# A decoder trunk on one core: the first layer's norm gain is put on the weights, and the first loads are issued in another order

## The chip, the cores and the metric

The kernel runs on one core of a Trainium2 chip. The time is the device time of one launch in microseconds (us). The engines are named as in the profile: PE is TensorE with its matmuls, PEld its weight loads, DVE is VectorE, ACT is ScalarE, POOL is GpSimd, SP is SyncE, which issues most of the DMAs.

## The reference

Four residual layers, each with an RMSNorm in front, over 256 tokens of width 1024, in float32. Layers 0 and 3 are a pooling mixer, layer 1 is a gated DeltaNet, layer 2 is latent attention.

```python
def rmsnorm(x, g):
    y = x * lax.rsqrt(jnp.mean(x * x, axis=-1, keepdims=True) + EPS)
    return y * g

def pool_mixer(h, w_in, w_grp, scale, w_out):       # w_in: 1024 x 4096
    u, gate = jnp.split(h @ w_in, 2, axis=-1)
    ...                                              # windowed means of u, one window per group
    return (p * scale * jax.nn.silu(gate)) @ w_out

for i in range(4):
    x = x + mixer[i % 3](rmsnorm(x, norm_g[i]), ...)
return rmsnorm(x, final_g)
```

The gain `g` multiplies the columns of `h`, and these are the rows of `w_in`. So `(y * g) @ w_in` is `y @ (g[:, None] * w_in)`.

## The kernel before

**Tiles.** The 256 tokens are two row tiles, `xs[0]` and `xs[1]` (128 partitions each, t=0 and t=1). The width of 1024 is eight blocks of 128 along the contraction, k=0 to 7. Every float32 operand of a matmul is split into two parts: `hi` is the value rounded to `fp32r`, `lo` the rest. One product is three matmuls: hi·hi, hi·lo, lo·hi.

**Weights** (`weights`, L97). A DMA on SP's queue brings `raw`, one k (256 KB) or two (512 KB). ACT writes `whi` with a copy that rounds (L117), DVE writes `wlo` as `raw - whi` (L119). For the k's in the list `pool` it is POOL that writes `wlo`. A ring holds nine pairs, and `raw` has three buffers. The weights of the first gate come one k at a time, k=0 to 5 through `prefetch`, k=6 and 7 in `project`.

**Norm** (`Normed`, `LayerIn`). ACT sums the squares (L209), POOL makes the factor `xr` of each row (L245, L247, L296). `gain_tile` loads the gain spread over all partitions, in two halves (L276). DVE writes `h = x * xr * gain` (L303). For t=1 POOL makes a part of it early as `hg = x * gain` (L291), and ACT puts the factor on it (L308). PE turns `h` (L323), ACT and DVE split it into `hTh` and `hTl` (L195, L200).

**The start.** PE does 24 transposes of `ident` (L270) while the loads come in. Then follows the gate of group 3 with the tokens on the partitions (L167: for each t, eight k's of three matmuls over 512 columns). All the later gates and `u` of layer 0 have the channels on the partitions (L127 to L129: 12 matmuls over 256 columns for each k).

**The gated DeltaNet of layer 1** (below: the GDN). `substitution` solves 32x32 triangles row by row on POOL, 31 pairs of L726 and L730, on data that DMAs bring from DRAM (`d_l` to `Lb`). The result `Tb` goes to DRAM as `d_t` (L732) and comes back as `T` in eight DMAs (L736). PE needs `T` in `pairs` (L806). While POOL works, PE does the input projections of the layer: `values` (turned at L778), `queries`, and the gate of group 2, called g2 below, with 48 matmuls of L167. Two of g2's `wlo` parts, k=3 and k=7, are made by POOL.

**Order.** A scheduler sets the order of instructions on each engine by a model of their times. The program gives dependencies, and `later(...)` names instructions after which something may be issued. So a change at the start can change the order far behind it.

Of the kernel before, what the change touches and what calls it, by code (L numbers as in the profile page):

```python
# [8 lines left out]
F32 = mybir.dt.float32  # L9
# [33 lines left out]
def trunk(ctx: ExitStack, tc: tile.TileContext, x, positions, norm_g, pool_w_in, pool_w_grp,  # L43
# [3 lines left out]
    nc = tc.nc  # L47
    PSUM = bass.MemoryType.PSUM

    WARM = 24  # L50
    FREE = 4
    EARLY = 6
    E0 = 2
# [19 lines left out]
    def worka(name, *dims):  # L73
        return wa.tile([P, *dims], F32, tag="wa", name=name)
# [7 lines left out]
    def bank(pool, name):  # L82
        return pool.tile([P, CW], F32, tag=name, name=name)
# [10 lines left out]
    ready = []  # L94
    held_back = {"free": 0, "after": []}

    def weights(src, n, cols, raw=None, pool=()):  # L97

        if raw is None:
            raw = rawp.tile([P, KU * CW], F32, tag="raw", name="raw")  # L100
        m = n * cols
        dst = raw[:, :m]
        if len(src.shape) == 3:
            dma = nc.sync.dma_start(out=dst.rearrange("p (k c) -> p k c", k=n), in_=src)
        else:
            dst = dst.rearrange("p (k a b) -> p k a b", k=n, a=src.shape[2])
            for k in range(n):
                dma = nc.sync.dma_start(out=dst[:, k], in_=src[:, k])
        parts = []
        for k in range(n):  # L110
            v = raw[:, k * cols:(k + 1) * cols]
            lo = ring.tile([P, CW], F32R, tag="wlo", name="wlo")[:, :cols]
            hi = ring.tile([P, CW], F32R, tag="whi", name="whi")[:, :cols]
            held = held_back["free"] <= 0
            held_back["free"] -= 1
            with later(*(held_back["after"] if held else ())):
                a = nc.scalar.copy(hi, v)  # L117
                e = nc.gpsimd if k in pool else nc.vector
                b = e.tensor_tensor(out=lo, in0=v, in1=hi.bitcast(F32), op=ALU.subtract)  # L119
# [9 lines left out]
        nc.tensor.matmul(o, lhsT=lhs[1], rhs=rhs[0], start=False, stop=stop)  # L129

    def project(src, ks, act, cols=CW, chan=False, tail=0, done=None, cuts=1,
                where="acc", pool=()):

        first, last = ks[0][0], sum(ks[-1]) - 1  # L140

        def unit(k0, n):
            return weights(src(k0, n), n, cols,
                           pool=[a for a in range(n) if (k0 + a) % KD in pool])

        if chan:
            banks = [bank(acc if where == "acc" else aux, where) for _ in range(2)]
            for k0, n in ks:
                parts = unit(k0, n)
                for j in range(n):  # L150
                    k = k0 + j
                    for c in range(cols // P):
                        w = [v[:, c * P:(c + 1) * P] for v in parts[j]]
                        o = banks[c // 2][:, (c % 2) * S:(c % 2 + 1) * S]
                        mm3(o, w, act(k, 0, S), k == first and c % 2 == 0,
                            k == last and c % 2 == 1)
            return banks
        width = cols // cuts
        banks = [[bank(acc, "acc") for _ in range(cuts)] for _ in range(NT)]

        def rows(t, c, k0, n, parts):
            o, sl = banks[t][c][:, :width], slice(c * width, (c + 1) * width)
            for x, y in ((0, 0), (0, 1), (1, 0)) if n == 1 else ((0, None), (1, 0)):
                for j in range(n):
                    k = k0 + j
                    for z in (0, 1) if y is None else (y,):
                        nc.tensor.matmul(o, lhsT=act(k, t * P, P)[x], rhs=parts[j][z][:, sl],  # L167
                                         start=k == first and x == z == 0,
                                         stop=k == last and x == 1)
# [83 lines left out]
    def load_x(t):  # L253
        for c in range(2):
            sl = slice(c * CW, (c + 1) * CW)
            nc.sync.dma_start(out=xs[t][:, sl], in_=x[0, t * P:(t + 1) * P, sl])

    load_x(0)
    neghalf = const.tile([P, 2], F32, name="neghalf")
    nc.gpsimd.memset(neghalf, -0.5)  # L260
# [5 lines left out]
    warm = small("warm", 2, bufs=1)  # L266
    nc.scalar.activation(warm, neghalf, AF.Silu)
    ps = bank(tps, "tp")
    for _ in range(WARM):
        nc.tensor.transpose(ps[:, :P], ident, ident)  # L270

    def gain_tile(row, between):
        g = gp.tile([P, D], F32, tag="gain", name="gain")
        for c in range(2):
            sl = slice(c * CW, (c + 1) * CW)
            nc.sync.dma_start(out=g[:, sl], in_=row[:, sl].to_broadcast([P, CW]))  # L276
            if c == 0 and between:
                between()
        return g

    class Normed:

        def __init__(self, row, between=None):
            self.g, self.early = gain_tile(row, between), {}

        def begin(self, t, a):
            sl = slice(a, a + CUT)
# [4 lines left out]
        def rest(self, t):  # L294
            r = small("xr", 1)
            mark["pool"] = nc.gpsimd.tensor_tensor(out=r, in0=ms[t], in1=neghalf[:, :1],  # L296
                                                   op=ALU.pow).ins
            hs = []
            for a in range(0, D, CW):
                h = wh.tile([P, CW], F32, tag="h", name="h")  # L300
                cut = CUT if (t, a) in self.early else 0
                sl = slice(a + cut, a + CW)
                nc.vector.scalar_tensor_tensor(out=h[:, cut:], in0=xs[t][:, sl], scalar=r[:, 0:1],  # L303
                                               in1=self.g[:, sl], op0=ALU.mult, op1=ALU.mult)
                hs.append(h)
                if not cut:
                    continue
                mark["rest"] = nc.scalar.activation(h[:, :CUT], self.early.pop((t, a)), AF.Copy,  # L308
                                                    scale=r[:, 0:1]).ins
            return hs  # L310

    class LayerIn(Normed):


        def __init__(self, i, between=None):
            super().__init__(norm_g[i:i + 1, :], between)
            self.hT = Split("hT", KD)

        def feed(self, t):
# [91 lines left out]
    def pool_layer(i, j, hT):  # L411
        yT = Split("yT", POOL_W // P)
        order = (3, 2, 1, 0)

        def gate(g):
            ks = [(k, 1) for k in range(KD)] if g == order[0] and i == 0 else units(KD)
            banks = project(cols_of(pool_w_in[j], POOL_W + g * CW), ks, hT, chan=g != order[0])
            gs = [worka("gs", CW) for _ in range(NT)]
            for t in range(NT):
                nc.scalar.activation(gs[t], banks[t], AF.Silu)  # L420
            return gs

        def pooled(g):
            w = WINDOWS[g]
            banks = project(cols_of(pool_w_in[j], g * CW), units(KD), hT, chan=True)
# [770 lines left out]
    def prefetch(k, pool=()):  # L1196
        ready.append(weights(first(k, 1), 1, CW, worka("raw", CW), pool))
# [12 lines left out]
    for k in range(1, E0):  # L1210
        prefetch(k)
    start(0)
    held_back["free"] = 0
# [39 lines left out]
```

## Time and profile before

| | us |
|---|---|
| median of 3 runs | 859.88 (859.83 to 860.01) |
| the profiled execution | 859.14 |
| its span in the trace | 857.4 |

The span is the time from the first to the last instruction in the trace; 1.7 us of the profiled execution lie around it. Times of the trace count from the span's start. In rows of the timeline stand start, length (the last to end of the merged ones), engine, line, operation, output and inputs, and in brackets how long the engine had been idle and what ended that.

### The profile page before, as it was taken

The page shows a single profiled execution, that of the slowest core. Times are in us where ns is not written, and L with a number is a line of the kernel's source. Part 1 is how long each engine was busy: PE and PEld are TensorE (multiplying, and loading weights), DVE is VectorE, ACT ScalarE, POOL GpSimd, SP SyncE. Part 2 cuts the span into 40 slices and gives each one's busy share as a digit, 9 for nine tenths or more (in the row PEclk, how much of TensorE's full clock was granted, in tenths as well). Part 3 has the DMA queues.
Part 4 walks back from the last instruction along what each step waited for, and adds up shares of the span by engine and source line. Part 5 has one row for each costly group of instructions (what it writes and reads, how often), then busy time and mean ns, then how long its engine had stood idle before and what let it go on. Part 6 is the DMA issues. An engine that isn't in the chain of part 4 may idle for free.

```text
span 857.4 us, 16137 instructions
## 1 busy us (share of the span) xinstructions
PE 835.0 (97%) x5967; PEld 778.7 (91%) x5967; DVE 591.2 (69%) x1138; ACT 488.2 (57%) x1007; POOL 155.7 (18%) x292
## 2 busy tenths in 40 slices
PE   7999999999999969999999999999999999999996
PEld 6999998988999959888979998999989989999986
DVE  4589776456989665656577659778767668866852
ACT  5565555467857435555565654566555476555542
POOL 4000000233248941022212002000000210000012
PEclk9999999999999989999999999999999999999999
DMA  6765556546555462222547676743652547565551
GB/s 199 249 188 188 178 189 213 180 148 206 188 160 176 134 168 102 75 74 99 173 147 215 201 165 172 196 132 95 171 167 79 173 149 218 175 192 183 187 200 50
DMA packets 111288, 140.43 MB, mean 164 GB/s; under 512 B 23340, under 2 KB 53224, under 8 KB 111208
## 3 DMA queue, kind: packets, MB, share of 16 engines
q1 hardware_dynamic: 109056, 138.17, 53.1%
q8 instruction: 47, 0.77, 0.4%
q0 software_dynamic: 320, 1.06, 0.3%
q10 hardware_dynamic: 1832, 0.16, 0.2%
q14 instruction: 33, 0.27, 0.1%
HBM read 137.79 MB, written 1.58 MB: 163 GB/s over the span
## 4 chain that ended last, share of the span: by engine, by line
PE 85%; POOL 7%; DVE 2%; DMA 2%; issue 2%; ACT 1%; SPq 1%; POOLq 0%; ACTq 0%; DVEq 0%
PE acc L167 34%; PE acc L127 12%; PE acc L128 12%; PE acc L129 12%; POOL Tb L730 2%; POOL pr L726 2%; PE aux L127 2%; PE aux L128 2%; PE aux L129 2%; DVE h L303 1%; DMA gain<-in_norm_g_dram 1%; PE aux L688 1%; ACT junk L209 1%; PE aux L806 1%; PE tp L1165 1%
## 5 line engine op out<-in xcount | busy, mean ns | idle before, releaser
L119 DVE TENSOR_TENSOR wlo<-raw,whi 128x512 fp32r<-128x512 f32 (+1 forms) x491 | 338.6, 712 | 163.2 <-ACT whi L117 160.9
L117 ACT CAST whi<-raw 128x512 fp32r<-128x512 f32 (+1 forms) x508 | 301.4, 617 | 261.8 <-PE acc L167 89.8
L127 PE MATMUL acc<-hTh,whi 128*128 128x256 f32 x832 | 235.3, 283 | 1.0 <-DVE cv L636 1.0
L128 PE MATMUL acc<-hTl,whi 128*128 128x256 f32 x832 | 235.8, 283 | 0.0
L129 PE MATMUL acc<-hTh,wlo 128*128 128x256 f32 x832 | 234.7, 282 | 0.0
L127 PEld LDWEIGHTS acc<-hTh,whi 128*128 128x128 f32 x832 | 157.7, 190 | 1.8 <-issue 1.4
L128 PEld LDWEIGHTS acc<-hTl,whi 128*128 128x128 f32 x832 | 157.6, 189 | 0.4
L129 PEld LDWEIGHTS acc<-hTh,wlo 128*128 128x128 f32 x832 | 157.5, 189 | 0.2
L167 PE MATMUL acc<-wlo,yTh 128*128 128x256 f32 (+1 forms) x384 | 116.2, 319 | 0.0
L167 PE MATMUL acc<-whi,yTh 128*128 128x256 f32 (+1 forms) x384 | 116.2, 323 | 0.0
L167 PE MATMUL acc<-whi,yTl 128*128 128x256 f32 (+1 forms) x384 | 92.4, 321 | 0.0
L167 PEld LDWEIGHTS acc<-wlo,yTh 128*128 128x128 f32 x384 | 72.0, 188 | 5.0
L167 PEld LDWEIGHTS acc<-whi,yTh 128*128 128x128 f32 x384 | 71.9, 188 | 5.2
L167 PEld LDWEIGHTS acc<-whi,yTl 128*128 128x128 f32 x384 | 63.1, 188 | 5.6
L291 POOL TENSOR_TENSOR hg<-x,gain 128x256 f32<-128x256 f32 x18 | 14.8, 832 | 259.1 <-DVE x L353 257.4
L167 PE MATMUL acc<-wlo,hTh 128*128 128x512 f32 (+1 forms) x144 | 55.9, 394 | 0.4 <-DVE wlo L119 0.2
L167 PE MATMUL acc<-whi,hTh 128*128 128x512 f32 (+1 forms) x144 | 55.5, 393 | 0.7 <-ACT hTh L195 0.7
L167 PE MATMUL acc<-whi,hTl 128*128 128x512 f32 (+1 forms) x144 | 45.4, 388 | 0.0
L119 POOL TENSOR_TENSOR wlo<-raw,whi 128x512 fp32r<-128x512 f32 x17 | 23.1, 1360 | 70.2 <-ACT whi L117 70.2
L434 POOL COPY win<-u 128x4 f32<-128x4 f32 x8 | 2.8, 354 | 177.0 <-ACT u L428 177.0
L167 PEld LDWEIGHTS acc<-wlo,hTh 128*128 128x128 f32 x144 | 27.3, 190 | 6.8 <-DVE wlo L119 1.7
L167 PEld LDWEIGHTS acc<-whi,hTh 128*128 128x128 f32 x144 | 27.3, 190 | 6.8 <-ACT hTh L195 1.7
(337 smaller groups left out, 1443.3 us busy)
## 6 DMA issues: line engine op xcount, KB each, us to landing
raw<-in_pool_w_in_dram SPq DMA_DIRECT2D x60, 512.0 KB, 4.4
raw<-in_gdn_w_in_dram SPq DMA_DIRECT2D x48, 512.0 KB, 3.9
raw<-in_pool_w_out_dram SPq DMA_DIRECT2D x32, 512.0 KB, 3.7
raw<-in_mla_w_in_dram SPq DMA_DIRECT2D x24, 512.0 KB, 4.4
raw<-in_mla_w_uq_dram SPq DMA_DIRECT2D x36, 256.0 KB, 3.8
raw<-in_pool_w_grp_dram SPq DMA_DIRECT2D x16, 512.0 KB, 4.2
raw<-in_gdn_w_out_dram SPq DMA_DIRECT2D x16, 512.0 KB, 3.5
raw<-in_mla_w_ukv_dram SPq DMA_DIRECT2D x32, 256.0 KB, 3.4
```

What stands on the lines that cost most here:

```text
L117: a = nc.scalar.copy(hi, v)
L119: b = e.tensor_tensor(out=lo, in0=v, in1=hi.bitcast(F32), op=ALU.subtract)
L127: nc.tensor.matmul(o, lhsT=lhs[0], rhs=rhs[0], start=start, stop=False)
L128: nc.tensor.matmul(o, lhsT=lhs[0], rhs=rhs[1], start=False, stop=False)
L129: nc.tensor.matmul(o, lhsT=lhs[1], rhs=rhs[0], start=False, stop=stop)
L167: nc.tensor.matmul(o, lhsT=act(k, t * P, P)[x], rhs=parts[j][z][:, sl], start=k == first and x == z == 0, stop=k == last and x == 1)
L209: nc.scalar.activation(junk[:, :n], src, AF.Square, scale=scale, accum_out=o)
L291: nc.gpsimd.tensor_tensor(out=self.early[t, a], in0=xs[t][:, sl], in1=self.g[:, sl], op=ALU.mult)
L303: nc.vector.scalar_tensor_tensor(out=h[:, cut:], in0=xs[t][:, sl], scalar=r[:, 0:1], in1=self.g[:, sl], op0=ALU.mult, op1=ALU.mult)
L688: nc.tensor.matmul(ps[:, b], lhsT=kT[hf][:, b, tt], rhs=rhs[hf][:, b, tt], start=True, stop=True)
L726: nc.gpsimd.tensor_tensor(out=pv, op=ALU.mult, in0=Lb[:, r, r + 1:, None].to_broadcast([M * Q, n, c]), in1=Tb[:, r:r + 1, :c].to_broadcast ...
L730: nc.gpsimd.tensor_tensor(out=tv, in0=tv, in1=pv, op=ALU.subtract)
```

## The change

For layer 0 the gain is no longer put on `h`. It is loaded as eight rows of 128 on ACT's DMA queue (`grow`), turned by PE between the warming transposes, and copied by DVE to `gain0`, one column for each k. ACT's rounding copy becomes an activation with that column as scale, and DVE's subtraction becomes `raw * gain - whi`. All splits of layer 0's input weights are done in this way: 8 k's in each of 8 groups, 64. POOL no longer takes the split of k=0. `h` of layer 0 is `x * xr` alone, for t=1 too. `gain_tile` is not called for layer 0. The loads on SP are kept in the order of the program: both halves of `x` for t=0, the weights k=0 to 3, `x` for t=1, then the other weights. Other layers keep their code.

```diff
-    WARM = 24
+    WARM = 22
+    GROW = 13
...
-                a = nc.scalar.copy(hi, v)
-                e = nc.gpsimd if k in pool else nc.vector
-                b = e.tensor_tensor(out=lo, in0=v, in1=hi.bitcast(F32), op=ALU.subtract)
+                if gains is not None:
+                    a = nc.scalar.activation(hi, v, AF.Copy, scale=gains[:, k:k + 1])
+                    b = nc.vector.scalar_tensor_tensor(out=lo, in0=v, scalar=gains[:, k:k + 1],
+                                                       in1=hi.bitcast(F32), op0=ALU.mult,
+                                                       op1=ALU.subtract)
+                else:
+                    a = nc.scalar.copy(hi, v)
+                    e = nc.gpsimd if k in pool else nc.vector
+                    b = e.tensor_tensor(out=lo, in0=v, in1=hi.bitcast(F32), op=ALU.subtract)
...
+    grow = const.tile([KD, P], F32, name="grow0")
+    nc.scalar.dma_start(out=grow, in_=norm_g[0].rearrange("(k p) -> k p", p=P))
     load_x(0)
...
-    for _ in range(WARM):
-        nc.tensor.transpose(ps[:, :P], ident, ident)
+    for n in range(WARM):
+        in_order(nc.tensor.transpose(ps[:, :P], ident, ident))
+        if n == GROW:
+            pg = bank(tps, "tp")
+            in_order(nc.tensor.transpose(pg[:, :KD], grow, ident[:KD, :KD]))
+            gain0 = const.tile([P, KD], F32, name="gain0")
+            gains_in = nc.vector.tensor_copy(gain0, pg[:, :KD]).ins
...
+                if self.g is None:
+                    with later(gains_in):
+                        nc.vector.tensor_scalar(h, xs[t][:, a:a + CW], r[:, 0:1], None, ALU.mult)
+                    hs.append(h)
+                    continue
...
-            for a in range(0, D, CW):
-                if t:
-                    nxt.begin(t, a)
             nxt.feed(t)
...
-    nxt = LayerIn(0, lambda: prefetch(0, (0,)))
-    for k in range(1, E0):
+    nxt = LayerIn(0)
+    for k in range(E0):
         prefetch(k)
```

**The order at the start.** SP's queue before (a row is a DMA; `x_93` is t=0, `x_94` is t=1):

```order
L256 DMA x_93<-in_x_dram 128x512 x2
L276 DMA gain<-in_norm_g_dram 128x512
L104 DMA raw<-in_pool_w_in_dram 128x512
L276 DMA gain<-in_norm_g_dram 128x512
L104 DMA raw<-in_pool_w_in_dram 128x512 x3
L256 DMA x_94<-in_x_dram 128x512 x2
L104 DMA raw<-in_pool_w_in_dram 128x512 x2
```

SP's queue now:

```order
L271 DMA x_93<-in_x_dram 128x512 x2
L110 DMA raw<-in_pool_w_in_dram 128x512 x4
L271 DMA x_94<-in_x_dram 128x512 x2
L110 DMA raw<-in_pool_w_in_dram 128x512 x4
L110 DMA raw<-in_pool_w_in_dram 128x2x512 x12
```

The two loads of the gain are gone, and the weights k=0 to 3 stand right behind `x` of t=0.

DVE's first rows before (`h` is the normed input, `wlo` a weight's low part, `hTl` that of the turned input):

```order
L303 SCALAR_TENSOR_TENSOR h<-x_93,xr,gain 128x512 x2
L119 TENSOR_TENSOR wlo<-raw,whi 128x512
L200 TENSOR_TENSOR hTl_169<-tp,hTh_168 128x4x128
L200 TENSOR_TENSOR hTl_178<-tp,hTh_177 128x4x128
L119 TENSOR_TENSOR wlo<-raw,whi 128x512 x2
L303 SCALAR_TENSOR_TENSOR h<-x_94,xr,gain 128x256 x2
L119 TENSOR_TENSOR wlo<-raw,whi 128x512
L200 TENSOR_TENSOR hTl_169<-tp,hTh_168 128x4x128
```

DVE's first rows now:

```order
L292 COPY gain_127<-tp 128x8
L323 TENSOR_SCALAR h<-x_93,xr 128x512 x2
L127 SCALAR_TENSOR_TENSOR wlo<-raw,gain_127,whi 128x512 x2
L215 TENSOR_TENSOR hTl_170<-tp,hTh_169 128x4x128
L215 TENSOR_TENSOR hTl_179<-tp,hTh_178 128x4x128
L127 SCALAR_TENSOR_TENSOR wlo<-raw,gain_127,whi 128x512 x6
L404 MEMSET rows 128x128
L323 TENSOR_SCALAR h<-x_94,xr 128x512 x2
```

All eight weight splits of the first gate now stand ahead of `h` of t=1; before, three did on DVE, with POOL's one. On PE all 24 matmuls of t=0 now come ahead of the transposes for t=1, where 12 did before.

**The order in the GDN.** No line of it is changed, but the scheduler moved its parts. POOL, in the second half of the substitution before (L726 and L730 are the chain, L119 the splits of g2 for k=3 and k=7):

```order
L730 TENSOR_TENSOR Tb<-Tb,pr 64x12x20
L119 TENSOR_TENSOR wlo<-raw,whi 128x512
L726 TENSOR_TENSOR pr<-Lb,Tb 64x231
L730 TENSOR_TENSOR Tb<-Tb,pr 64x11x21
L726 TENSOR_TENSOR pr<-Lb,Tb 64x220
L730 TENSOR_TENSOR Tb<-Tb,pr 64x10x22
L726 TENSOR_TENSOR pr<-Lb,Tb 64x207
L730 TENSOR_TENSOR Tb<-Tb,pr 64x9x23
L726 TENSOR_TENSOR pr<-Lb,Tb 64x192
L119 TENSOR_TENSOR wlo<-raw,whi 128x512
L730 TENSOR_TENSOR Tb<-Tb,pr 64x8x24
```

POOL at the end of the substitution now (L754 and L758 are the chain, L133 the splits):

```order
L133 TENSOR_TENSOR wlo<-raw,whi 128x512
L754 TENSOR_TENSOR pr<-Lb,Tb 64x135
L758 TENSOR_TENSOR Tb<-Tb,pr 64x5x27
L754 TENSOR_TENSOR pr<-Lb,Tb 64x112
L758 TENSOR_TENSOR Tb<-Tb,pr 64x4x28
L754 TENSOR_TENSOR pr<-Lb,Tb 64x87
L758 TENSOR_TENSOR Tb<-Tb,pr 64x3x29
L754 TENSOR_TENSOR pr<-Lb,Tb 64x60
L758 TENSOR_TENSOR Tb<-Tb,pr 64x2x30
L754 TENSOR_TENSOR pr<-Lb,Tb 64x31
L133 TENSOR_TENSOR wlo<-raw,whi 128x512
L758 TENSOR_TENSOR Tb<-Tb,pr 64x31
```

The first split stood ahead of step 64x231 of the chain and stands now ahead of step 64x135, six pairs of steps later; the second stood within step 64x192 and stands now within the last step.

SP's queue around the way of `T` through DRAM before:

```order
L104 DMA raw<-in_gdn_w_in_dram 128x2x512 x15
L732 DMA d_t<-Tb 64x1024
L104 DMA raw<-in_gdn_w_in_dram 128x2x512
L736 DMA T<-d_t 32x8x32 x8
L104 DMA raw<-in_gdn_w_in_dram 128x2x512 x2
```

And now:

```order
L110 DMA raw<-in_gdn_w_in_dram 128x2x512 x13
L760 DMA d_t<-Tb 64x1024
L764 DMA T<-d_t 32x8x32
L110 DMA raw<-in_gdn_w_in_dram 128x2x512
L764 DMA T<-d_t 32x8x32 x4
L110 DMA raw<-in_gdn_w_in_dram 128x2x512
L764 DMA T<-d_t 32x8x32 x3
L110 DMA raw<-in_gdn_w_in_dram 128x2x512 x3
```

Two weight loads fewer are issued ahead of `d_t`, and two stand between the loads of `T`. On PE, between the last matmul of L688 (which feeds the substitution) and L806, 299 matmuls of L127 to L129 and the 48 of g2 stood before; now it is 276 and the 48. The other 23 come behind L806.

More of the change, by code (lines that the diff above doesn't have):

```diff
@@ L95, in trunk, with in_order, weights @@
     held_back = {"free": 0, "after": []}
-    def weights(src, n, cols, raw=None, pool=()):
+    def in_order(ins):
+        return tc.keep_in_program_order(ins)
+    def weights(src, n, cols, raw=None, pool=(), gains=None):
         if raw is None:
@@ L104, in weights @@
             dma = nc.sync.dma_start(out=dst.rearrange("p (k c) -> p k c", k=n), in_=src)
+            if gains is not None:
+                in_order(dma)
         else:
@@ L131, in project @@
     def project(src, ks, act, cols=CW, chan=False, tail=0, done=None, cuts=1,
-                where="acc", pool=()):
+                where="acc", pool=(), gains=None):
         first, last = ks[0][0], sum(ks[-1]) - 1
@@ L143, in unit @@
             return weights(src(k0, n), n, cols,
-                           pool=[a for a in range(n) if (k0 + a) % KD in pool])
+                           pool=[a for a in range(n) if (k0 + a) % KD in pool],
+                           gains=None if gains is None else gains[:, k0:k0 + n])
         if chan:
@@ L255, in load_x @@
             sl = slice(c * CW, (c + 1) * CW)
-            nc.sync.dma_start(out=xs[t][:, sl], in_=x[0, t * P:(t + 1) * P, sl])
+            in_order(nc.sync.dma_start(out=xs[t][:, sl], in_=x[0, t * P:(t + 1) * P, sl]))
+    grow = const.tile([KD, P], F32, name="grow0")
+    nc.scalar.dma_start(out=grow, in_=norm_g[0].rearrange("(k p) -> k p", p=P))
     load_x(0)
@@ L268, in trunk, with gain_tile @@
     ps = bank(tps, "tp")
-    for _ in range(WARM):
-        nc.tensor.transpose(ps[:, :P], ident, ident)
-    def gain_tile(row, between):
+    for n in range(WARM):
[5 more added lines that the diff above has]
+            gains_in = nc.vector.tensor_copy(gain0, pg[:, :KD]).ins
+    def gain_tile(row):
         g = gp.tile([P, D], F32, tag="gain", name="gain")
@@ L276, in gain_tile, with __init__ @@
             nc.sync.dma_start(out=g[:, sl], in_=row[:, sl].to_broadcast([P, CW]))
-            if c == 0 and between:
-                between()
         return g
     class Normed:
-        def __init__(self, row, between=None):
-            self.g, self.early = gain_tile(row, between), {}
+        def __init__(self, row):
+            self.g, self.early = None if row is None else gain_tile(row), {}
         def begin(self, t, a):
@@ L312, in trunk, with __init__ @@
     class LayerIn(Normed):
-        def __init__(self, i, between=None):
-            super().__init__(norm_g[i:i + 1, :], between)
+        def __init__(self, i):
+            super().__init__(norm_g[i:i + 1, :] if i else None)
             self.hT = Split("hT", KD)
@@ L413, in pool_layer @@
         order = (3, 2, 1, 0)
+        gains = None if i else gain0
         def gate(g):
             ks = [(k, 1) for k in range(KD)] if g == order[0] and i == 0 else units(KD)
-            banks = project(cols_of(pool_w_in[j], POOL_W + g * CW), ks, hT, chan=g != order[0])
+            banks = project(cols_of(pool_w_in[j], POOL_W + g * CW), ks, hT, chan=g != order[0],
+                            gains=gains)
             gs = [worka("gs", CW) for _ in range(NT)]
@@ L424, in pooled @@
             w = WINDOWS[g]
-            banks = project(cols_of(pool_w_in[j], g * CW), units(KD), hT, chan=True)
+            banks = project(cols_of(pool_w_in[j], g * CW), units(KD), hT, chan=True, gains=gains)
             u = big("u", 4, S)
@@ L1194, in trunk, with prefetch @@
     first = cols_of(pool_w_in[0], POOL_W + (len(WINDOWS) - 1) * CW)
-    def prefetch(k, pool=()):
-        ready.append(weights(first(k, 1), 1, CW, worka("raw", CW), pool))
+    def prefetch(k):
+        ready.append(weights(first(k, 1), 1, CW, worka("raw", CW), gains=gain0[:, k:k + 1]))
     def start(t):
```

1 line of the change is left out of this document (added).

## The prediction

> **What bounds the kernel now.** I read the page's busy shares and its chain first, then PE's waits, then the timeline of the two places where PE waits.
>
> ```profile
> span 857.4 us, 16137 instructions
> PE 835.0 (97%) x5967; PEld 778.7 (91%) x5967; DVE 591.2 (69%) x1138; ACT 488.2 (57%) x1007; POOL 155.7 (18%) x292
> PE 85%; POOL 7%; DVE 2%; DMA 2%; issue 2%; ACT 1%; SPq 1%; POOLq 0%; ACTq 0%; DVEq 0%
> ...
> PE aux L806 <- DMA T<-d_t: 7.4, 1, 7.4
> PE tp L323 <- DVE h L303: 3.0, 2, 1.6
> PE tp L323 <- ACT h L308: 1.0, 1, 1.0
> ```
>
> PE is the bound, 97% busy. A gain must come from the 22.4 us without PE, or from matmuls at less than full clock. POOL's 7% of the chain is the substitution in the GDN, ended by the longest wait, 7.4 us. The waits at L323 are the start. The span is 857.4, the execution 859.14, the median 859.88; I work out differences in the trace and put them on the median.
>
> ```profile
> 1.96 5.15 PE L270 MATMUL tp<-ident 128*128 128x128 f32 x24 [1.96 <-POOL ident masks.py:199]
> 3.46 0.63 ACT L209 ACTIVATE junk<-x 128x512 f32<-128x512 f32 x1 [1.17 <-DMA x<-in_x_dram]
> 5.36 0.57 POOL L296 TENSOR_TENSOR xr<-ms,neghalf 128x1 f32<-128x1 f32 x1
> 7.63 0.75 DVE L303 SCALAR_TENSOR_TENSOR h<-x,xr,gain 128x512 f32<-128x512 f32 x1 [7.63 <-DMA gain<-in_norm_g_dram]
> 8.19 0.62 ACT L117 CAST whi<-raw 128x512 fp32r<-128x512 f32 x1 [3.25 <-DMA raw<-in_pool_w_in_dram]
> 8.44 0.66 PE L323 MATMUL tp<-ident,h 128*128 128x128 f32 x4 [1.34 <-DVE h L303]
> 9.16 1.53 DVE L303 SCALAR_TENSOR_TENSOR h<-x,xr,gain 128x512 f32<-128x512 f32 x1 [0.78 <-DMA gain<-in_norm_g_dram]
> 10.27 0.58 ACT L195 CAST hTh<-tp 128x512 fp32r<-128x512 f32 x1
> 11.51 0.78 PE L167 MATMUL acc<-whi,hTh 128*128 128x512 f32 x1
> 16.49 1.10 PE L323 MATMUL tp<-ident,h 128*128 128x128 f32 x8 [1.01 <-ACT h L308]
> 17.39 0.98 PE L167 MATMUL acc<-whi,hTh 128*128 128x512 f32 x2
> 18.67 0.40 PE L167 MATMUL acc<-whi,hTl 128*128 128x512 f32 x1
> 18.91 0.40 PE L167 MATMUL acc<-whi,hTh 128*128 128x512 f32 x1
> ```
>
> The reader sees that the row factor is ready at 5.93, but `h` starts at 7.63 and 9.16, when the gain's halves land. From 17.39 PE always has work. By then it has done 12 of the 48 matmuls of the first gate.
>
> **The start, worked out.** Removed: two gain loads (256 KB each), two `hg` on POOL, two `h` halves on ACT, a 1.26 us split on POOL, two warming transposes. Added: one 4 KB load, one small transpose, one copy.
>
> PE warms until about 6.8 (22 transposes of 0.215 from 1.96, and the small one). `h` needs the factor (5.93) and `gain0`. For that I need the new load and the landing of the weights:
>
> ```profile
> raw<-in_pool_w_in_dram SPq DMA_DIRECT2D x8, 256.0 KB, 6.1
> x<-in_x_dram SPq DMA_DIRECT2D x4, 256.0 KB, 4.6
> L1047 DVE TENSOR_SCALAR ckv<-ckv,mrr 128x512 f32<-128x512 f32 x2 | 0.9, 475 | 0.0
> L200 DVE TENSOR_TENSOR yTl<-ym,yTh 128x256 fp32r<-128x256 f32 x16 | 6.7, 418 | 0.8 <-ACT yTh L195 0.5
> L202 DVE SCALAR_TENSOR_TENSOR yTl<-tp,colsT,yTh 128x256 fp32r<-128x256 f32 x24 | 10.4, 477 | 4.9 <-ACT yTh L197 4.8
> 60.00:80.00 20.00, 20.00 (x149) 18.90 (x148) 18.84 (x36) 13.32 (x25) 2.00 (x3) 1.00 0.56 177
> ```
>
> `grow`, issued at about 0.85, lands between 3.4 (the first `x`, 3.46, took 2.6 from the start of issue) and 7.0 (6.1 after issue, as weights do). I take 4, as nothing is ahead of it. Its transpose comes after 14 warming ones, at 4.97, so `gain0` is there at 5.4. With 7.0, PE's last eight warm until 8.8: 2.0 later.
>
> Then: `h` 5.95 to 6.9 (two of 0.475; before 0.75 and 1.53). Transposes 6.8 to 7.9. Weights k=0, 1 land right behind `x`, 5 to 6 (at the latest 1.71 + 6.1 = 7.8), ACT splits them before `hTh` at 7.45 and 8.05. First matmul at about 8.05, against 11.51. From there DVE sets the pace: `hTl` until 9.35, then six splits of 0.65. Those for k=4 to 7 come at the earliest 2.6 after their issue, which waits for the split of k=0 (7.5): 10.1, at the latest 13.6. I take 11. The last split ends at 14.5 to 15.4 and PE's t=0 at about 15.2. `h` of t=1 is behind the eight splits on DVE and its squares behind three on ACT: 14.6 to 15.5. Transposes, the SiLU of t=0 and three DMA issues stand ahead of `hTh` on ACT. PE is then at work without a break from 16.6 to 17.1.
>
> Sum: 17.39 less 16.85 is 0.55. PE has done 24 matmuls instead of 12, at 0.235 (18.67 to 18.91) 2.8. The first five after 17.39 took 1.28 instead of 0.94: 0.3. Start: **-3.65**. With the late landings (2.0 or 2.6 more) it is -1.2, with the early ones -4.6.
>
> What is late next at the start is DVE with the splits, then PE itself. SP passes two gain issues less, 0.9 us.
>
> **The splits of layer 0.** 64 become scalar_tensor_tensor. On 128x256 this takes 477 against 418 ns, so I add 0.06 each, 3.8 us on DVE in all; ACT's activation with a scale I take at the same. The tightest stretch is 60 to 80: DVE is busy 18.84 of 20. A k lasts PE 12 x 0.119 = 1.43, so 14 splits add 0.84, and 1.16 are free. The ring of nine covers delays within. Cost 0 to 0.84 (3.8 if nothing covered), I take 0.2.
>
> **The GDN, which only moves.** All times here are those of before; the earlier start shifts them together.
>
> ```profile
> 291.55 0.40 PE L167 MATMUL acc<-whi,hTh 128*128 128x512 f32 x1
> 293.13 1.28 POOL L119 TENSOR_TENSOR wlo<-raw,whi 128x512 fp32r<-128x512 f32 x1
> 295.05 0.40 PE L167 MATMUL acc<-wlo,hTh 128*128 128x512 f32 x1
> 298.81 1.29 POOL L119 TENSOR_TENSOR wlo<-raw,whi 128x512 fp32r<-128x512 f32 x1
> 302.86 0.82 POOL L730 TENSOR_TENSOR Tb<-Tb,pr 64x156 f32<-64x156 f32 x1
> 303.76 0.83 POOL L726 TENSOR_TENSOR pr<-Lb,Tb 64x135 f32<-64x135 f32 x1
> 262.99 0.42 POOL L726 TENSOR_TENSOR pr<-Lb,Tb 64x135 f32<-64x135 f32 x1
> 309.54 0.23 POOL L726 TENSOR_TENSOR pr<-Lb,Tb 64x31 f32<-64x31 f32 x1
> 310.12 0.47 SPq L732 DMA_DIRECT2D d_t<-Tb  x1
> 313.12 3.78 SPq L736 DMA_DIRECT2D T<-d_t  x8
> 308.45 0.28 PE L129 MATMUL acc<-hTh,wlo 128*128 128x256 f32 x1
> 316.09 3.65 PE L806 MATMUL aux<-T,LT 128*128 128x64 f32 x16 [7.36 <-DMA T<-d_t]
> 316.10:324.40 8.30, 8.30 (x41) 8.30 (x41) 4.88 (x6) 3.13 (x8) 0.00 (x0) 0.51 0.68 205
> 324.40:332.00 7.60, 7.60 (x75) 7.60 (x72) 4.67 (x9) 5.67 (x14) 0.00 (x0) 1.00 0.13 38
> ```
>
> The reader sees POOL's chain end at 310.1, `T` after it, and PE idle from 308.7 to 316.09; then 8.3 us at a granted clock of 0.51, which cost another 4.1.
>
> Now POOL comes to the split of k=3 only after the step that ended at 303.68; without the two splits, that is 301.1, so it is done at 302.4. PE wants it 3.5 us into g2, at 295.05, or some 2.5 later where `values` are turned earlier than now. So PE gets a **new wait of 5 to 7 us on POOL**, then 24 matmuls (5.6, to 308.0), a second wait for k=7 until 309.8 (309.54 + 0.23, the two splits counted within), 9 matmuls and 16 smaller ones (4.0), and the rest of the wait for `T`. POOL's chain holds the same work, so `T` comes at 316.1, plus one load between its first four, 0.45. Behind the waiting PE nothing but its own work is queued; ACT and DVE wait for its turned tiles.
>
> Price, part by part. 23 matmuls of 0.119 move behind L806, where PE is full: +2.7. `T` later: +0.5. The idle time is now in three pieces with work between, the last about 2.3, so I expect the slow clock before L806, where the wait for `T` hides it: -4.1 (0 if it comes again). Weight loads that stood ahead of `d_t` come behind it, and turned tiles are freed on ACT behind those weights: a load takes 4, and PE has 1.3 of work there, so I add 2.5 (0 to 3). DVE is idle in this stretch for want of weights, and POOL was faster then: 0.42 for step 64x135 at 262.99, 0.83 at 303.76. Some ten steps at 0.1 to 0.3 less: -1 (0 to -3). GDN: **+0.6**, between -2.5 and +5.
>
> The Trainium skill ("TensorE: Matmul & The Clock Gate", section "Part 1: The HAM clock gate (the "warmup" mystery)") gives the half clock after at least one idle window of about 3.4 us, and the full one after a busy window as long. The trace has it after a longer wait than that, 7.36, and for longer, 8.3. By the rule the new wait of 5 us alone would halve the clock, which falls into time that `T` hides; my sum would be the same. It would change only where the last piece exceeds 3.4, the second rival.
>
> Layers 2 and 3 and the output keep their code and, but for local exchanges, their order; I take 0, within 0.5.
>
> Sum: -3.65 + 0.2 + 0.6 = -2.85, **857.0 us**.
>
> **Rivals.**
> - *The GDN gives too.* Speaks for it: POOL's fast steps. Then GDN is -2.0 instead of +0.6, 854.4.
> - *Slower: the new waits on POOL cost the clock twice.* The last wait for `T` is long as well, and L806 again runs at half clock (4.1), with two weight loads ahead of the second half of `T` (0.9). GDN +5.6, sum +2.15, 862.0. It decides from a GDN price of 3.45 on; speaks for it that this wait did halve the clock before; against it that work now stands between.
> - *Late loads.* The gain rows or the weights k=4 to 7 land as late as 6.1 after issue. Start -1.2, 859.5. Speaks for it the row of the eight weight loads; against it that these stood behind the gain, which is gone.
> - *The gain's wait was hidden.* PE's matmuls start earlier, but are done no sooner, as DVE's eight splits set the pace: start -0.55, 860.1. Against it: then PE would wait between them, and the 2.8 of work done are still done.
>
> **Chances.** 857.0: 0.46. GDN gives too: 0.19. Late loads: 0.17. Hidden wait: 0.08. Slower: 0.10. The range of the likeliest is 855.5 to 858.5. The range for 8 in 10 runs from 854.0 (the second case's 854.4 less the 0.5 of the other layers) to 860.4, above the third and fourth case. A change of 0.2%, 1.7 us, is about what can be told from none: faster is below 858.16. The first two cases are faster but for 0.03, the late loads fall within: faster 0.65, same 0.26, slower 0.09.
>
> **What would show it.** In the profile after: no gain row ahead of `h`, the first L182 at about 8, PE without a break from about 17 with all of t=0 behind it. A wait of PE on POOL's `wlo` of 4 us or more in g2. L806 within 2 us of its old distance from L688, at full clock. PE's waits in layer 0 stay below 1. I am wrong if the first matmul comes after 10, if L806 runs at 0.5, or if layer 0 shows waits on `wlo` of over 2 us.

## The result: 873.9 us, slower by 1.7%, and the profile after

| | us | ratio to before |
|---|---|---|
| before | 859.86 | |
| after | 873.9 (873.3 to 874.0) | 1.0168 (1.0152 to 1.0184) |
| profiled execution after | 873.31, span 871.6 | |

A fourth run of the changed kernel took 1655.86 us, in a slow state that no profile shows, and is left out of the range and the ratio.

The forecast was 857.0 with 860.4 as its upper end. The time lies 13.5 us above that. The start became faster, as forecast; all of the loss lies in layers 1 and 2, whose code is not touched.

The page after: the line of the span, the busy shares, and the shares of the chain that ended last.

```profile
span 871.6 us, 16132 instructions
...
PE 840.2 (96%) x5966; PEld 777.4 (89%) x5966; DVE 596.4 (68%) x1140; ACT 494.4 (57%) x1005; POOL 152.4 (17%) x289
...
PE 63%; POOL 7%; DMA 3%; DVE 3%; ACT 2%; issue 2%; SPq 0%; POOLq 0%; ACTq 0%; DVEq 0%
```

PE is without work for 31.4 us (871.6 less 840.2) instead of 22.4. That explains 9 of the 14 us. The other 5 stand in PE's row as busy. Nearly 3 of them lie in the state chain and layer 2, where PE counts as busy 1.1 and 1.8 us longer for as many matmuls (821 and 1470, before 823 and 1470) at the full granted clock; I take them for waits shorter than the view shows. The rest lies ahead of the state chain, in part at half clock behind the first wait below. The longest waits of PE after (line waited for: total, times, longest):

```profile
PE acc L141 <- DVE vc L664: 4.7, 1, 4.7
PE aux L834 <- DMA T<-d_t: 4.5, 1, 4.5
PE tp L287 <- POOL ident masks.py:199: 2.0, 1, 2.0
PE acc L182 <- DVE wlo L133: 1.8, 3, 1.0
PE aux L897 <- ACT gsg L584: 1.7, 1, 1.7
PE tp L943 <- DVE yg L934: 1.6, 1, 1.6
...
PE acc L182 <- POOL wlo L133: 1.3, 1, 1.3
```

The waits for `h` at the start are gone. A wait of 4.7 on `vc` is new: `vc` is what DVE's convolution makes of the products of `values`, and PE waits until it has read a bank of `acc`. New too are waits of 1.7 and 1.6 in the state chain, the part of the GDN behind the substitution that goes head by head (`state`, `unseen`, `second`, `output`; its products stand in `aux`).

The start after, in PE's timeline:

```profile
5.13 0.27 PE L290 MATMUL tp<-ident,grow 8*128 8x8 f32 x1
...
6.93 1.04 PE L349 MATMUL tp<-ident,h 128*128 128x128 f32 x8
8.21 0.50 PE L182 MATMUL acc<-whi,hTh 128*128 128x512 f32 x1 [0.24 <-ACT hTh L210]
...
15.07 0.50 PE L182 MATMUL acc<-whi,hTh 128*128 128x512 f32 x1 [0.37 <-ACT whi L126]
...
16.43 1.04 PE L349 MATMUL tp<-ident,h 128*128 128x128 f32 x8
17.82 0.50 PE L182 MATMUL acc<-whi,hTh 128*128 128x512 f32 x1 [0.35 <-ACT hTh L210]
```

The first matmul of the gate is at 8.21 instead of 11.51, and all 24 of t=0 are done before t=1 is turned.

Where time is won and lost is seen from five marks on PE: the first matmul of L595 (layer 1; L567 before), the first with `T` (L834), the first of the state chain (L897), the first turn of `ckv` (layer 2), the last four turns of `h` (layer 3). The table gives their starts in the trace before, and how much later (+) or earlier (-) they are in the others; e1 to e4 and e10 are kernels of the next section.

| | layer 1 | T | state chain | layer 2 | layer 3 | span |
|---|---|---|---|---|---|---|
| before | 183.42 | 316.09 | 359.55 | 490.31 | 695.36 | 857.4 |
| after | -2.5 | -0.2 | +3.1 | +9.8 | +14.3 | +14.2 |
| e1, new, banks 6 and 4 | -2.3 | -2.3 | -3.4 | -3.4 | -3.3 | -3.4 |
| e2, old, banks 4 and 2 | -0.1 | -3.8 | +6.3 | +12.2 | +16.7 | +16.7 |
| e3, new, banks 4 and 4 | -2.0 | +0.6 | +2.5 | +2.5 | +3.9 | +3.9 |
| e4, new, banks 6 and 2 | -3.0 | -1.6 | -1.4 | +2.6 | +9.7 | +9.0 |
| e10, old, two banks of tp | +0.9 | -1.0 | +7.6 | +13.9 | +18.0 | +18.1 |

Each trace is of a single run: e1's took 1.1 us less than the median of its kernel, e10's 3.0 more, the others at most 0.8 off.

Layer 0 gives 2.5. The GDN up to `T` loses 2.3, from there to the state chain 3.3 (26 matmuls more stand there, 329 against 303), the state chain and what follows to layer 2 6.7, layer 2 4.5; layer 3 and the output nothing.

### The profile page after: what moved, and what is told of

Same layout as the page of the kernel before. It is cut to its first block, busy times and chain, and to the rows that moved or that the text cites. A ratio compares the mean times of both kernels' runs of the same rounds, so it can differ in the third digit from the quotient of the medians.

```text
span 871.6 us, 16132 instructions
## 1 busy us (share of the span) xinstructions
PE 840.2 (96%) x5966; PEld 777.4 (89%) x5966; DVE 596.4 (68%) x1140; ACT 494.4 (57%) x1005; POOL 152.4 (17%) x289
## 4 chain that ended last, share of the span: by engine, by line
PE 63%; POOL 7%; DMA 3%; DVE 3%; ACT 2%; issue 2%; SPq 0%; POOLq 0%; ACTq 0%; DVEq 0%
PE acc L182 24%; PE acc L142 9%; PE acc L143 9%; PE acc L141 9%; POOL pr L754 2%; POOL Tb L758 2%; PE aux L141 1%; PE aux L142 1%; PE aux L143 1%; DVE wlo L133 1%; ACT junk L224 1%; PE aux L716 1%; PE aux L834 1%; DMA raw<-in_pool_w_in_dram 1%; PE tp L1193 1%
## 5 line engine op out<-in xcount | busy, mean ns | idle before, releaser
L131 ACT CAST whi<-raw 128x512 fp32r<-128x512 f32 (+1 forms) x444 | 264.3, 617 | 240.2 <-PE acc L182 93.0
L133 DVE TENSOR_TENSOR wlo<-raw,whi 128x512 fp32r<-128x512 f32 (+1 forms) x428 | 295.4, 713 | 149.7 <-ACT whi L131 145.1
L182 PE MATMUL acc<-whi,yTh 128*128 128x256 f32 (+1 forms) x384 | 114.1, 323 | 1.7 <-ACT yTh L212 1.4
L182 PE MATMUL acc<-whi,yTl 128*128 128x256 f32 (+1 forms) x384 | 89.8, 319 | 0.0
L126 ACT ACTIVATE whi<-raw,gain 128x512 fp32r<-128x512 f32 x64 | 44.5, 722 | 28.0 <-DMA raw<-in_pool_w_in_dram 11.0
L127 DVE SCALAR_TENSOR_TENSOR wlo<-raw,gain,whi 128x512 fp32r<-128x512 f32 x64 | 46.4, 748 | 13.5 <-ACT whi L126 12.0
```

Of the source, the lines that this page charges most:

```text
L126: a = nc.scalar.activation(hi, v, AF.Copy, scale=gains[:, k:k + 1])
L127: b = nc.vector.scalar_tensor_tensor(out=lo, in0=v, scalar=gains[:, k:k + 1], in1=hi.bitcast(F32), op0=ALU.mult, op1=ALU.subtract)
```

## The cause: how many PSUM banks each pool may use

PSUM is the memory that PE writes its products to, and a bank holds one tile of 128x512 here. The kernel writes no number of buffers for its three PSUM pools `tp` (turned tiles), `acc` (projections) and `aux` (all else). A planner in the build chooses them, within eight banks. It begins with the fewest banks with which the program can run at all, and raises the limits of those pools that hold work up in its model. A pool may share its banks with another when the other needs none, so the limits can add up to more than eight.

| the build's report | tp | acc | aux | sum |
|---|---|---|---|---|
| before, first step | 1 | 4 | 2 | 7 |
| before, final | 2 | 6 | 4 | |
| after, first step and final | 2 | 4 | 2 | 8 |

The change brings a small transpose (L290) between the warming ones, with a bank of `tp` of its own. The warming transposes behind it still write to theirs. So two banks of `tp` must exist from the first step on, all eight are taken, and no PSUM pool has room to be raised. The one limit that the planner then tried to raise, that of `hg`, bought nothing in its model, and it stopped at 2, 4 and 2. The order of layers 1 and 2, which I had read as the scheduler's answer to an earlier start, is its answer to these limits.

What two banks of `aux` less do in the state chain is seen in 31 us of it, before, after and in e1 (stretch and its length; busy time and count of PE, PEld, DVE, ACT and POOL; granted clock, DMA share, GB/s):

```profile
359.50:390.50 31.00, 30.94 (x149) 26.06 (x148) 18.60 (x41) 19.15 (x56) 8.45 (x24) 1.00 0.17 52
```

```profile
362.70:393.70 31.00, 26.43 (x121) 20.57 (x121) 16.43 (x35) 14.64 (x42) 5.33 (x16) 1.00 0.16 52
```

```profile
356.00:387.00 31.00, 30.94 (x148) 26.07 (x147) 18.51 (x41) 19.25 (x56) 8.45 (x24) 1.00 0.16 52
```

PE does 121 matmuls instead of 149 in the same time, and no engine is busier for it. I read it so: each step of a head waits until DVE, ACT or POOL have emptied a bank. The view names such waits only in part (in e4, where `aux` alone is small, one of 0.6 on DVE's `vn`, two of 0.5 on `st`, one of 0.4 on `yg`); that they go with the limit is shown by e1 and e4.

What two banks of `acc` less do is seen around 266 us after. First PE's rows at the wait, then four of DVE's rows in it, then the windows (the granted clock is the third number from the end):

```profile
265.06 0.28 PE L143 MATMUL acc<-hTh,wlo 128*128 128x256 f32 x1
270.06 0.55 PE L141 MATMUL acc<-hTh,whi 128*128 128x256 f32 x1 [4.72 <-DVE vc L664]
270.41 0.42 PE L142 MATMUL acc<-hTl,whi 128*128 128x256 f32 x1
```

```profile
265.85 1.29 DVE L133 TENSOR_TENSOR wlo<-raw,whi 128x512 fp32r<-128x512 f32 x2 [0.34 <-ACT whi L131]
267.06 1.65 DVE L664 SCALAR_TENSOR_TENSOR vc<-acc,tap,vc 128x254 f32<-128x254 f32 x4
268.62 0.90 DVE L133 TENSOR_TENSOR wlo<-raw,whi 128x512 fp32r<-128x512 f32 x1
269.44 1.64 DVE L664 SCALAR_TENSOR_TENSOR vc<-acc,tap,vc 128x253 f32<-128x253 f32 x4
```

```profile
266.00:268.00 2.00, 0.00 (x0) 0.00 (x0) 2.00 (x5) 2.00 (x6) 2.00 (x4) 1.00 0.61 230
268.00:270.00 2.00, 0.00 (x0) 0.00 (x0) 2.00 (x5) 0.31 (x1) 1.84 (x5) 0.90 0.77 219
270.00:272.00 2.00, 1.94 (x9) 1.97 (x10) 2.00 (x6) 1.26 (x2) 1.76 (x4) 0.50 0.11 43
272.00:274.00 2.00, 2.00 (x15) 2.00 (x15) 2.00 (x6) 0.10 (x1) 1.76 (x4) 0.75 0.00 0
```

PE has no bank for the next product until DVE has run the convolution on the last one, between splits of weights. Behind the wait come some 3 us at half clock. The wait is there in all kernels with 4 banks for `acc` (4.7 in e2 and e10, 5.4 in e3), and in none with 6.

The Trainium skill ("Perfetto Trace Analysis", section "Matmul Optimizations") advises to use all eight PSUM banks. Both kernels do by the build's report, 16384 bytes of each partition; the runs show that the share of each pool decides too.

## The experiments

**e1: the change with the old limits.**

```diff
-    acc = ctx.enter_context(tc.tile_pool(name="acc", space=PSUM))
+    acc = ctx.enter_context(tc.tile_pool(name="acc", bufs=6, space=PSUM))
-    aux = ctx.enter_context(tc.tile_pool(name="aux", space=PSUM))
+    aux = ctx.enter_context(tc.tile_pool(name="aux", bufs=4, space=PSUM))
```

> The changed kernel with the limits of its PSUM pools written down as the planner had chosen them for the kernel before: at most 6 banks for acc and 4 for aux (in the changed kernel the planner had chosen 4 and 2). Theory P (the loss comes from the two smaller limits, which reorder layers 1 and 2): the order of layers 1 to 3 on every engine is that of before again, so the lead of 2.5 us with which layer 1 begins in the trace after is kept to the end: 859.9 - 2.5 = 857.4, within 0.7; PE's wait of 4.7 on DVE's vc and the waits in the state chain are gone, the wait for T is 7 us again. Rival S (layer 0's scaled splits or the earlier start disturb what follows, whatever the banks): stays at 868 or above, as the lead had been lost by 316 us before the state chain began.

856.8, ratio 0.9966 (0.9953 to 0.9979). Theory P holds: behind layer 0 the order is that of before but for a few rows, the new waits are gone, and `T` is waited for as before:

```profile
PE aux L834 <- DMA T<-d_t: 7.2, 1, 7.2
PE tp L287 <- POOL ident masks.py:199: 2.0, 1, 2.0
PE acc L182 <- ACT hTh L210: 1.3, 5, 0.3
PE acc L141 <- DVE cv L664: 0.8, 1, 0.8
```

**e2: the kernel before with the small limits** (`bufs=4` and `bufs=2`, nothing else).

> The kernel before with the two smaller limits, 4 banks for acc and 2 for aux, and nothing of the change. Theory P: all of the loss behind layer 0 comes without the change: in the trace after, the lead at layer 1 was 2.5 and the end 14.3 behind, so 16.7 are lost; 859.9 + 16.7 = 876.6, within 2, with the loss in the same places (by the wait for T 2.3, from there to the end of layer 1 10, in layer 2 4.4). Rival S: stays within 3 us of 859.9.

875.2, ratio 1.0173 (1.0155 to 1.0192). The loss comes without the change. Its places are those expected but for `T`, which came earlier here (-3.8); the 10.1 between `T` and the state chain take that back.

**e3 and e4: one limit each** (`acc` 4 with `aux` 4, and `acc` 6 with `aux` 2).

> The changed kernel with 4 banks for acc and 4 for aux: only aux is given back. Theory A (aux, which holds the products of the GDN's state chain and of the heads of layer 2, carries the losses there): the 7.4 lost between 357 and 402 and the 4.4 of layer 2 come back, 873.9 - 11.8 = 862.1, within 2. Theory C (acc carries them, because the projections that fill PE's time run out of banks): 868 to 872.

> The changed kernel with 6 banks for acc and 2 for aux: only acc is given back. Theory A: the losses of the state chain and of layer 2 stay, and what is lost before the wait for T and from there to 357 (2.3 + 2.8) may come back: 869 to 874. Theory C: 860 to 864.

862.8 (1.0029, 1.0019 to 1.0039) and 868.3 (1.0095, 1.0080 to 1.0111). Against e1, the small `acc` costs 6.0 and the small `aux` 11.5, together 17.5; both at once cost 17.1 (873.9 less 856.8). In e3 the loss lies ahead of the state chain and only 1.4 in layer 2; in e4 it is the state chain (4.0) and layer 2 (7.1). Theory A is right on the larger part; e4 came out 0.7 below its range of 869 to 874.

**e10 and e9: the one bank.** In e10 the kernel before writes one of its 24 warming transposes to a second bank. In e9 the change's small transpose gets free columns of the first.

```diff
-        nc.tensor.transpose(ps[:, :P], ident, ident)
+        nc.tensor.transpose((ps2 if n == 14 else ps)[:, :P], ident, ident)
```

> The kernel before with one edit: one of the 24 warming transposes writes to a second bank of tp. Nothing of the change is in it, and no transpose more is done. Theory B: the planner starts with two banks for tp, stays at 4 and 2 for acc and aux, and the time is that of the kernel before with these limits, 875.2 within 1.5. Rival S: 859.3 within 1, as one transpose's target is nothing.

```diff
-            pg = bank(tps, "tp")
+            pg = ps[:, P:]
```

> The changed kernel as it is, with no limit written down, but the small transpose of the gain goes into free columns of the bank of the warming transposes instead of a bank of its own. Theory B (the second bank of tp that must exist beside the first at the start is what fills the eight PSUM banks at the planner's first step, so that it cannot raise acc and aux): the planner comes to 6 and 4 by itself, and the time is that of the changed kernel with these limits, 856.8 within 0.7. Rival S (the loss is in what the change does to the work of layer 0): 868 or above.

e10: 874.2, ratio 1.0176 (1.0155 to 1.0197). e9: 857.4, ratio 0.9973 (0.9963 to 0.9984), with limits 2, 6 and 4 chosen by the planner itself. The target of one transpose moves the time by 14.6 us without the change (from 859.6) and by 16.5 with it (from 873.9). Theory B holds both ways; rival S is excluded.

**e6: the scaled splits.** All 64 splits of layer 0 are made by the plain copy and subtraction (`if gains is not None` becomes `if False` there). This kernel leaves out the gain of layer 0.

> The changed kernel with 6 and 4 banks, in which the gain of layer 0 is left out (its weights are split by the plain copy and subtraction; all else as in the change). It measures what the scaled splits cost against 856.8. The forecast's term was 0.2, with 0 to 0.84 as bounds: 856.0 to 856.8. Rival: the scaled splits hold PE in 60 to 80 us, where DVE is 19.5 of 20 busy, and cost 1.2 or more: 855.6 or less.

856.7, ratio 0.9974 (0.9966 to 0.9983), against e1's 0.9966. The scaled splits cost nothing that these intervals can tell from zero; the rival's 855.6 or less is excluded.

**e8: only the new order of the loads**, in the kernel before (limits written down as 2, 6 and 4). The loads on SP are kept in the new order, and the two gain loads go to ACT's queue; the cut shows the second part.

```diff
-            nc.sync.dma_start(out=g[:, sl], in_=row[:, sl].to_broadcast([P, CW]))
+            q = nc.scalar if between else nc.sync
+            q.dma_start(out=g[:, sl], in_=row[:, sl].to_broadcast([P, CW]))
```

> The kernel before, gain still on the input, with only the loads in the new order: both halves of x, the weights k=0 to 3, x of t=1, the other weights on SP, and the two gain loads on ACT's queue; limits of the PSUM pools as before (6, 4 and 2). Theory L (the order of the loads gives the start, the algebra adds little): h no longer waits beyond the row factor and the time is 857.3, within 0.7. Theory G (the 512 KB of the gain still land ahead of the weights, and POOL's and ACT's parts of h stay): 858.4 to 859.6.

859.9, ratio 1.0009 (1.0000 to 1.0018), 0.3 above the range of theory G. Nothing is gained, and not because `h` waits for the gain: it waits for the row factor, as `x` is late. The gain's 512 KB are issued on ACT's queue beside `x`, and ACT's squares wait for the halves of `x` until 5.27 and 7.42 (the first 3.46 before), POOL's factor is ready at 9.13 (5.93 before), and `h` starts behind it. PE waits 4.68, and turns `h` at half clock (1.97 for eight, 1.04 after the change):

```profile
5.27 0.63 ACT L211 ACTIVATE junk<-x 128x512 f32<-128x512 f32 x1 [2.54 <-DMA x<-in_x_dram]
7.42 0.63 ACT L211 ACTIVATE junk<-x 128x512 f32<-128x512 f32 x1 [1.43 <-DMA x<-in_x_dram]
9.17 2.41 DVE L307 SCALAR_TENSOR_TENSOR h<-x,xr,gain 128x512 f32<-128x512 f32 x2 [9.17 <-POOL xr L300]
10.97 1.97 PE L327 MATMUL tp<-ident,h 128*128 128x128 f32 x8 [4.68 <-DVE h L307]
```

So this order alone does not give the start while the gain is loaded in full beside `x`. An order with the gain's loads behind `x` was not tried.

**e5, e11, e12: what limits the start now.** e5 gives the raw weights two more buffers, e11 puts the squares and `h` of t=1 ahead of the splits of k=4 to 7, e12 does both.

```diff
+    held_back["after"] = [extra["sq"], extra["h"]]
     for k in range(E1, EARLY):
```

> The changed kernel with 6 and 4 banks, and with two buffers more for the raw weights of the first gate, so that the loads of k=4 and 5 need not wait for the split of k=0 (SP stood from 4.5 to 7.48 for it). Against the one without these buffers (856.8). Theory W (the waiting issue is what made PE's unbroken work begin at 18.08 instead of the 16.85 of the forecast): it begins between 16.3 and 17.1, and the time is 855.3 (854.8 to 855.9). Rival D (the DMA engines are the limit, 0.9 busy from 4 to 12 us): k=7 lands no sooner than 0.5 before 15.8, and the time stays at 856.3 to 857.3.

> The changed kernel with 6 and 4 banks, in which the squares and h of t=1 stand ahead of the splits of k=4 to 7 on ACT and DVE. Against 856.8. Theory H (h of t=1, behind eight splits on DVE, is what PE's second half of the gate waits for): t=1 is turned at about 13 instead of 16.7, the matmuls of t=1 for k=0 to 3 fill PE's gaps before 18, some 3 us in all, and part of that is gained: 855.3, between 854.6 and 856.0. Rival D (the loads of k=4 to 7 set the pace): 856.3 to 857.5.

> The same with the two more buffers for the raw weights of the first gate, which alone brought nothing (857.0). If both h of t=1 and the loads hold PE at the start, only the two together pay: PE's waits between 8 and 18 us, 3.5 in all, fall to 1.5 or less, and the time is 854.9, between 854.2 and 855.8. If the loads are bounded by the DMA engines: within 0.5 of the one without the buffers.

857.0 (0.9978, 0.9966 to 0.9990), 856.7 (0.9964, 0.9952 to 0.9977) and 855.6 (0.9956, 0.9944 to 0.9969). The 855.3 of theory W (e5) and of theory H (e11) did not come; e12 lies in its range. The 15.8 in the expectation of e5 is the split of the next gate's first load. That of k=7 waited for its load until 14.55 in e1, and in e5 the four splits of k=4 to 7 run from 11.40 to 14.15: the load of k=7 came sooner, but PE's unbroken work began at 18.17, as `h` of t=1 stands behind the splits. Each alone moves the wait: PE's rows of e5 and of e11 at the turn of `h`, or behind it:

```profile
16.84 1.09 PE L350 MATMUL tp<-ident,h 128*128 128x128 f32 x8 [1.04 <-DVE h L324]
```

```profile
12.79 1.09 PE L352 MATMUL tp<-ident,h 128*128 128x128 f32 x8 [0.41 <-DVE h L325]
...
17.31 0.50 PE L183 MATMUL acc<-whi,hTh 128*128 128x512 f32 x1 [1.77 <-ACT hTh L211]
```

With both, PE's busy time from 8 to 20 us is 11.30, against 10.11 in e1, and layer 1 begins at 179.28 instead of 181.15. Of these 1.9, 0.8 are left when `T` comes (312.92 against 313.75). e12 has the lowest time of all kernels here, below both that were given; but its interval overlaps those of e1, e5 and e11.

**e7: g2's two splits off POOL** (`(3, 7)` becomes `()` in the list of `gate`).

> The changed kernel with 6 and 4 banks, in which the two splits of the gate g2 (k=3, k=7) are made by DVE instead of POOL. Theory T (POOL's chain sets when T comes, and T is what PE waits for): the chain ends 2.6 us sooner (2 x 1.29) and PE's wait of 7.2 for T shrinks by it; one split that now stands behind the chain and some 8 matmuls moved behind L834 (1.0) take part of it back: 856.8 - 1.6 = 855.2, between 854.2 and 856.0. Rival: the splits are late on DVE, or T's loads are held by weight loads, and PE waits there instead: 856.5 or more.

857.0, ratio 0.9975 (0.9966 to 0.9984): the rival's number, by another way than it said.

```profile
312.31 3.65 PE L834 MATMUL aux<-T,LT 128*128 128x64 f32 x16 [8.68 <-DMA T<-d_t]
```

`T` came 1.4 sooner than in e1, but PE ran out of work sooner too, and its wait grew from 7.17 to 8.68. Behind `T`, up to the state chain, stand 324 matmuls now instead of 303 in e1, and they are paid there: that stretch takes 45.63 instead of 42.40. An earlier `T` is worth only what PE's idle time shrinks.

## Why the forecast was wrong, point by point

- **The step that failed** is "Layers 2 and 3 and the output keep their code and, but for local exchanges, their order; I take 0, within 0.5", together with "The GDN, which only moves". I read the new order from the listing and priced its waits one by one, but never asked how many banks stood behind it. The runs show 17.1 us for the limits. In the trace after, 4.5 are lost in layer 2 alone, where I took 0, and 6.7 from the start of the state chain to layer 2, for which the sum of the GDN has no term.
- **The start** was right in kind and too large: -3.65 forecast, -2.5 and -2.3 measured at layer 1 (after and e1). `h` began at 5.93 (forecast 5.95), the first matmul at 8.21 (8.05). PE's unbroken work began at 17.82 instead of 16.85. The mis-sized term is the landing of k=4 to 7: I took 11, and ACT's split of k=7 waited for a DMA until 14.29, later than the 13.6 that I had as the latest:

```profile
14.29 0.72 ACT L126 ACTIVATE whi<-raw,gain 128x512 fp32r<-128x512 f32 x1 [0.55 <-DMA raw<-in_pool_w_in_dram]
```

- **The splits**, 0.2 forecast: e6 finds nothing that can be told from zero. That agrees, but 0.2 is less than the runs can tell.
- **The GDN up to `T`.** The new wait on POOL in g2 was to be 5 to 7; it was 1.3, because PE came late to it, after the wait of 4.7 on `vc` that I had not seen. POOL's chain took 48.75 instead of 50.31 (-1.6; forecast -1, 0 to -3). But the way of `T` got longer by 3.4, where I took one issue, 0.45: 4.07 instead of 3.00 from `d_t` to the first load of `T`, and 5.32 instead of 2.97 from there to L834. SP's rows after:

```profile
306.52 0.46 SPq L760 DMA_DIRECT2D d_t<-Tb  x1
310.59 0.34 SPq L764 DMA_DIRECT2D T<-d_t  x1
311.02 0.41 SPq L110 DMA_DIRECT2D raw<-in_gdn_w_in_dram  x1
311.47 1.94 SPq L764 DMA_DIRECT2D T<-d_t  x4
```

  A 512 KB load stands behind the first of `T`'s eight small ones and another behind the fifth. The small ones landed 3.5 to 4.9 us after their issue, before the change 1.8 to 2.1, so they waited for more than the 0.45 of an issue; that it is for the large load's data is the likely reading, not shown. The time from the first load to L834 is 5.20 in e3, with the same row order; in before, e1, e2, e4 and e7, where the eight follow one another, 2.80 to 3.05. The Trainium skill ("DMA: Bandwidth & Descriptors", section "Two DMAs through the same engine are not ordered") says that the descriptors within one queue of one DMA engine start in order; the rows agree.

  Of the terms behind `T`, the 2.7 for 23 moved matmuls held: that stretch takes 3.3 more, with 26 matmuls more. The 2.5 for late weight loads does not show in it.
- **The half clock** that was to be saved came twice, behind the wait on `vc` and behind `T`. That is in part the mechanism of the slower rival, which stood at 0.10: L834 ran at half clock again, 3.65 for 16, with two weight loads between those of `T`. But the first halving came from the wait on `vc`, not from one on POOL, and its 862.0 was far too little, as it knew nothing of what lies behind `T`.
- With the loss to the limits taken out, as in e1 and e9, the time is 856.8 and 857.4. That the forecast of 857.0 lies between them is partly chance: the start gave 1.2 to 1.4 less, and the GDN's +0.6 did not come, since its order stayed.

## What to carry to other kernels

Where a planner chooses the numbers of buffers, compare these numbers before and after a change ahead of any timing argument: a pool whose least need rises by one can take away the room of others that are far from the edit. A listing that shows another order in untouched code is a symptom; ask which resource the scheduler lost. Such limits are better written down once a good set is known, and small helpers at the start should use memory that is there already.

## What the runs showed of the hardware

The half clock also follows waits shorter than the 7.36 of before, and its delay varies. After a wait of 4.45 for `T` it began about 2.5 us after PE's last matmul and lasted until 324:

```profile
310.00:312.00 2.00, 1.46 (x13) 1.26 (x11) 1.09 (x2) 1.12 (x2) 0.00 (x0) 1.00 0.11 18
312.00:314.00 2.00, 0.00 (x0) 0.00 (x0) 0.00 (x0) 0.00 (x0) 0.00 (x0) 0.99 0.77 218
314.00:316.00 2.00, 0.09 (x1) 0.12 (x1) 0.00 (x0) 0.56 (x2) 0.00 (x0) 0.50 0.94 206
...
322.00:324.00 2.00, 2.00 (x12) 2.00 (x11) 0.41 (x1) 1.10 (x4) 0.00 (x0) 0.50 0.70 195
324.00:326.00 2.00, 2.00 (x23) 2.00 (x22) 0.00 (x0) 2.00 (x7) 0.00 (x0) 0.95 0.18 68
```

Before, it began 5.2 us after PE's last matmul (308.7 to 313.9). In all these runs the clock was halved during or soon after every wait of PE of 3.5 us or more, the shortest one of 3.52 at the start of e10. Below that the length of one wait does not decide: the waits of 1.7 and 1.6 in the state chain after were not followed by half clock. In e2 the wait for `T` was 1.43. The 16 matmuls of L806 behind it still took 1.97 instead of 3.65, but then the clock was halved for 3.41 us, although PE had been busy for 2.02 of the 3.42 us before:

```profile
310.86:314.28 3.42, 2.02 (x18) 2.04 (x19) 2.59 (x5) 2.60 (x6) 0.00 (x0) 1.00 0.49 78
314.28:317.69 3.41, 3.41 (x18) 3.41 (x17) 2.72 (x4) 0.45 (x1) 0.00 (x0) 0.50 0.82 246
```

The stretches at half clock inside the program last 3.41 us (here), 6.82 (e3, from 316.33), 10.24 (after, from 313.96) or 13.65 (e7, from 306.17), one to four times the same length. The Trainium skill ("TensorE: Matmul & The Clock Gate", section "Part 1: The HAM clock gate (the "warmup" mystery)") gives a window of about 3.4 us that runs freely; these lengths and the changing delay agree. The idle window after which it halves the clock need not be one without any work, if it ends where the clock falls: that in e2 was more than half busy.

Not tried: filling PE's wait for `T` with transposes, and keeping the loads of `T` together with the small limits, since each moved other work as well.
